# Low parts of 34 expert blocks made beside the mixers and kept in DRAM; the delta heads' inverse by transposes

## The chip, the core and the metric

The kernel runs on one core of one Trainium2 chip. The metric is device microseconds of one execution. TensorE (PE) multiplies matrices, VectorE (DVE) and ScalarE (ACT) work elementwise, GpSimd (POOL) and SyncE (SP) mainly issue DMAs here, and all DMAs run on the core's 16 DMA engines. Each engine takes its instructions strictly in order, and so does the queue in which SP or POOL issues DMAs: an issue that waits holds back every issue behind it.

## The reference, cut to what matters

One decoder layer for 544 tokens (512 of a prompt, 32 of samples). Two token mixers run on the projections of the normalised input; one of them, the gated delta rule, solves a unit triangular system for each chunk and head. Then comes a product-key expert layer with 16,384 experts of one neuron each.

```python
def gated_delta_recurrence(q, k, v, g, beta, s0):
    ...
        lmat = jnp.where(strict, bt[..., :, None] * gam * kk, 0.0)
        rhs = bt[..., None] * (vc.transpose(0, 2, 1, 3) - eg[..., None] * ks)
        u = lax.linalg.triangular_solve(eye + lmat, rhs, left_side=True, lower=True,
                                        unit_diagonal=True)

def peer_ffn(h, peer_wq, peer_keys, expert_u, expert_v):
    ...
        idx = ia * N_KEYS + ib                       # 128 experts chosen for each token
        gate = jax.nn.softmax(s_top, axis=-1)
        u = expert_u[idx]
        act = jax.nn.gelu(jnp.einsum('nd,nhkd->nhk', hb, u).astype(F32))
        wgt = (gate * act).astype(hb.dtype)
        return jnp.einsum('nhk,nhkd->nd', wgt, expert_v[idx])
```

## The kernel before, in words

**High and low parts.** A float32 matrix that TensorE is to multiply is split into a high part `whi` (rounded to the matmul's format) and a low part `wlo` (the rest), and a product is made of three matmuls: high by high, high by low, low by high. `wload` (lines 125 to 135) loads a block of 128 x 1024 through SP into `wraw`, ACT copies it to `whi` (line 120), and DVE subtracts to get `wlo` (line 121). `wsum` (lines 136 to 145) spares DVE: ACT writes `whi` (line 142) and then minus `whi` into `wlo` (line 143), and a DMA that POOL issues (line 144) adds the block from DRAM onto it once more.

**Mixers (83 to about 540 us).** The loop over the four heads (line 746 on) steps three generators side by side: `mix_a` (HGRN2 head), `mix_b` (delta head) and a filler that makes the next head's projections (`proj`, the matmuls of line 153) or the gates. What each step emits is then ordered on the engines by a scheduler; `order` rows below show the outcome. In `mix_b`, `inverse` builds the inverse of I + L for four chunks at once by doubling: at each of six levels, L times XT (line 532) is masked into ZT (533), then X times ZT (536) is subtracted from XT (540), and, except at the last level, ZT times X (539) is subtracted from X (542). XT is the transpose of X all along. All these are float32 matmuls of 128 x 128, and their PSUM tiles come from a pool `mb` of two buffers.

**Early expert blocks (750 to about 1140 us).** The expert inputs `eu` are 128 blocks of 128 experts. For 384 of the tokens the kernel computes all activations densely: `dots_u` makes 24 matmuls of 384 columns per block (lines 931, 932, 934) into `pu`. 62 blocks run early: the first 28 (`NPRE`) stay in SBUF, and 34 (`NSP`, every second block from 29 on) are stored to DRAM (`asp`, line 946) and read back later. All 62 take their weights through `wsum`, with three `wraw` and four `whi` and `wlo` buffers. Up to 922 us this runs beside the top-16 selection, which is DVE work; then `gates_of` (lines 1027 to 1056) builds, for 12 groups of 32 tokens, a dense map of the gates: one-hot tiles `oa` and `ob` on DVE and ACT, their product `pg` on TensorE (1048), a copy to `go` on ACT (1050, two buffers), a product on DVE (1052), and four DMAs that SP issues to store `go` into `gdram` (1056). Between them, rows of `eur` and `ev` for the other tokens are gathered by indirect DMAs that POOL issues (1073), and DVE multiplies them (1081, 1091).

**Product phase (1190 to 1970 us).** The remaining 66 blocks and all products with `ev` (line 1159).

The order of the expert part is that of a scheduler that simulates the engines; the mixers' order comes from a scheduler too.

Of the kernel before, what the change touches and what calls it, by code (L numbers as in the profile page):

```python
# [18 lines left out]
T = 544  # L19
# [17 lines left out]
NH2 = 4  # L37
NSP = 34
SEL = (0, 1, 2, 4, 3)
LATE = 127  # L40
XL, NYO = 118, 6
TW = 3, 2
# [9 lines left out]

@with_exitstack
def step_kernel(ctx: ExitStack, tc: tile.TileContext, xT, pT, pk, wab, win, wbr, wout, wq, keysT, eu, eur, ev,
                wple, wpg, sh, sd, scv, yT, o_hp, o_dp, o_cv, o_hs, o_ds, gdram, ysp, gsp, x1s, asp):
    nc = tc.nc
    V, S, G, PE = nc.vector, nc.scalar, nc.gpsimd, nc.tensor

# [77 lines left out]
    def wsum(src):  # L136

        raw = wr.tile([128, 1024], F32, name="wraw", tag="wraw", bufs=NRAW)
        nc.sync.dma_start(raw, src)
        hi = wp.tile([128, 1024], F32R, name="whi", tag="whi", bufs=NHI)  # L140
        lo = wp.tile([128, 1024], F32R, name="wlo", tag="wlo", bufs=NHI)
        S.activation(hi, raw, AF.Copy)
        S.activation(lo, hi.bitcast(F32), AF.Copy, scale=-1.0)
        G.dma_start(lo, src, accum_op=OP.add)
        return hi.rearrange("p (k c) -> p k c", c=128), lo.rearrange("p (k c) -> p k c", c=128)

    def mm3(ps, pairs, halves=(0, 1)):
# [322 lines left out]
    def mix_b(h):  # L470
# [36 lines left out]
        def bc(mk, n):  # L507
            return mk[:, None, :].to_broadcast([128, 4, 128]) if n == 4 else mk[:NS, :NS]

        def inverse(Lm, X, XT, ZT, n, levels):  # L510
            def each(f):
                if n == 4:
                    for c in range(4):
                        f(lambda t: t[:, c])
                else:
                    f(lambda t: t)

            def ps():
                p = p4()
                return p if n == 4 else p[:NS, 0, :NS]  # L520

            idt = ident if n == 4 else ident[:NS, :NS]
            p = ps()
            each(lambda at: PE.transpose(at(p), at(Lm), idt))
            V.tensor_mul(ZT, p, bc(maskf[1], n))
            V.tensor_sub(XT, bc(ident, n), ZT)
            V.tensor_mul(X, Lm, bc(m1l, n))
            V.tensor_sub(X, bc(ident, n), X)
            yield
            for m in levels:  # L530
                p = ps()
                each(lambda at: PE.matmul(at(p), at(Lm), at(XT), start=True, stop=True))  # L532
                V.tensor_mul(ZT, p, bc(maskf[m], n))
                yield
                p2 = ps()
                each(lambda at: PE.matmul(at(p2), at(X), at(ZT), start=True, stop=True))  # L536
                if m != levels[-1]:
                    p3 = ps()
                    each(lambda at: PE.matmul(at(p3), at(ZT), at(X), start=True, stop=True))
                V.tensor_sub(XT, XT, p2)  # L540
                if m != levels[-1]:
                    V.tensor_sub(X, X, p3)
                yield

        X, XT, ZT = m4("m2"), m4("m3"), m4("m4")
# [130 lines left out]
    def gates(c0, n):  # L676
        for c in range(c0, c0 + n):
# [2 lines left out]
            G.dma_start(gsp[:, c], sg)  # L680
            yield

    def chain(*gs):
        for g_ in gs:
            yield from g_
# [58 lines left out]
    for h in range(NH):  # L744
# [6 lines left out]
        while any(alive):  # L751
# [3 lines left out]
            if i % FP[h] == 2 or not alive[1]:  # L755
                alive[2] = next(fill, 0) is None
            i += 1
    nc.sync.dma_start(o_cv, ncv)
    mixers.close()
    mp = yinA.enter_context(tc.tile_pool(name="mg", bufs=2, side="right", reuse_waits="tile"))  # L760
# [155 lines left out]


    acts = {}
    spilled = [NPRE + 1 + 2 * i for i in range(NSP)]
    early = list(range(NPRE)) + spilled  # L920
    act = ap_.tile([128, NPRE, ND], F32, name="act", bufs=1)
    slots = []
# [13 lines left out]

    def ublock_early(j):
        with tc.high_priority(offset=100000):
            wh, wl = wsum(eu[j])
        ps = dots_u(wh, wl)  # L940
        a = act[:, j] if j < NPRE else stored(j)
        S.activation(a, ps[:, :ND], AF.Gelu_apprx_tanh)  # L942
# [387 lines left out]
             o_hs=(4, 128, 8, 128), o_ds=(4, 128, 8, 128))  # L1330


_SCR = dict(gdram=(128, NGQ, ND // 32, 128), ysp=(128, 8, T), gsp=(128, 16, T), x1s=(5, 128, 8, 128), asp=(NSP, 128, ND))


def unlay(np, r):
# [27 lines left out]
```

## Time and profile before

| | us |
|---|---|
| median of three runs (2071.32 to 2079.03) | 2077.46 |
| the profiled execution's own time | 2075.1 |
| its span | 2073.3 |
| mixers, 83 to 540: PE, DVE, ACT busy | 455.22, 339.26, 245.11 of 457 |
| selection, 770 to 920: PE, DVE busy | 147.30, 149.86 of 150 |
| gate maps, 922 to 1188: PE, DVE, ACT busy | 231.60, 224.08, 166.81 of 266 |
| product phase, 1190 to 1970: PE busy | 780.00 of 780 |

The page lists busy time, idle time and its releaser for each engine. A view of stretches gives, for a stretch of the span, each engine's busy time, the granted clock of TensorE (1.00 is its upper level), the mean busy share of the 16 DMA engines and GB/s. A DMA share slightly over 1 is one in which the engines were never without a packet. A matmul's duration overlaps its successor's; its price is the distance between two starts.

### The profile page before, as it was taken

The page shows a single profiled execution, that of the slowest core. Times are in us where ns is not written, and L with a number is a line of the kernel's source. Part 1 is how long each engine was busy: PE and PEld are TensorE (multiplying, and loading weights), DVE is VectorE, ACT ScalarE, POOL GpSimd, SP SyncE. Part 2 cuts the span into 40 slices and gives each one's busy share as a digit, 9 for nine tenths or more (in the row PEclk, how much of TensorE's full clock was granted, in tenths as well). Part 3 has the DMA queues.
Part 4 walks back from the last instruction along what each step waited for, and adds up shares of the span by engine and source line. Part 5 has one row for each costly group of instructions (what it writes and reads, how often), then busy time and mean ns, then how long its engine had stood idle before and what let it go on. Part 6 is the DMA issues. An engine that isn't in the chain of part 4 may idle for free.

```text
span 2073.3 us, 34544 instructions
## 1 busy us (share of the span) xinstructions
PE 1981.1 (96%) x12372; PEld 1841.1 (89%) x12372; DVE 1677.8 (81%) x4534; ACT 1004.9 (48%) x1660; POOL 547.4 (26%) x537
## 2 busy tenths in 40 slices
PE   6999999999998999998989799999999999999986
PEld 6899999998997999998989688888888888888886
DVE  7776968785566999998889898888888888887877
ACT  5646465643344357765767333333333333333374
POOL 0001010101000001134444455543434343443500
PEclk9999999999998999999999899999999999999998
DMA  4112131222754259999999999999999998999843
GB/s 150 62 42 83 59 106 47 89 89 92 270 178 138 78 123 242 241 280 325 304 324 329 309 357 340 337 352 345 347 341 350 331 344 329 337 337 335 292 133 105
DMA packets 178573, 480.46 MB, mean 232 GB/s; under 512 B 17376, under 2 KB 70624, under 8 KB 178272
## 3 DMA queue, kind: packets, MB, share of 16 engines
q1 hardware_dynamic: 117264, 257.63, 36.2%
q0 software_dynamic: 61136, 220.62, 33.0%
q8 instruction: 97, 1.59, 0.3%
q14 instruction: 76, 0.62, 0.1%
HBM read 435.82 MB, written 42.37 MB: 231 GB/s over the span
## 4 chain that ended last, share of the span: by engine, by line
PE 80%; issue 5%; DVE 5%; DMA 4%; ACT 3%; SPq 2%; POOL 0%; DVEq 0%; ACTq 0%; POOLq 0%
PE pacc L1159 25%; PE pj L153 14%; PE pu L931 7%; PE pu L932 7%; PE pu L934 7%; PE pj L881 4%; PE pj L1268 2%; SPq L1056 2%; PE pg L1048 2%; DMA gdram<-go 1%; PE pma L336 1%; PE pmb L532 1%; PE pmb L536 1%; DMA rows<-in_ev,idxs 1%; PE psc L902 1%
## 5 line engine op out<-in xcount | busy, mean ns | idle before, releaser
L931 PE MATMUL pu<-hh,whi 128*128 128x384 f32 x1024 | 346.8, 339 | 9.5 <-ACT acts L942 6.8
L932 PE MATMUL pu<-hl,whi 128*128 128x384 f32 x1024 | 346.0, 338 | 0.0
L1073 POOL DMA_INDIRECT rows<-in_ev,idxs x160 | 219.1, 1369 | 260.0 <-DVE accg L1091 221.3
L120 ACT ACTIVATE whi<-wraw 128x1024 fp32r<-128x1024 f32 x172 | 181.5, 1056 | 192.8 <-PE pj L153 93.7
L121 DVE TENSOR_TENSOR wlo<-wraw,whi 128x1024 fp32r<-128x1024 f32 x172 | 209.9, 1221 | 79.6 <-ACT whi L120 67.9
L1073 POOL DMA_INDIRECT rows<-in_eur,idxs x160 | 206.1, 1288 | 241.3 <-DVE jk L1081 192.5
L1091 DVE SCALAR_TENSOR_TENSOR accg<-rows,wts,accg 128x1024 f32<-128x1024 f32 x158 | 202.2, 1280 | 14.9 <-DMA rows<-in_ev,idxs 14.5
L931 PEld LDWEIGHTS pu<-hh,whi 128*128 128x128 f32 x1024 | 193.1, 189 | 13.3 <-ACT acts L942 7.1
L934 PE MATMUL pu<-hh,wlo 128*128 128x384 f32 x1024 | 204.5, 337 | 0.0
L1159 PE MATMUL pacc<-whi,wgl 128*128 128x512 f32 x768 | 197.3, 392 | 4.7 <-DVE wgl L121 4.6
L1159 PE MATMUL pacc<-whi,wgh 128*128 128x512 f32 x768 | 197.8, 393 | 3.7 <-ACT wgh L120 3.7
L1159 PE MATMUL pacc<-wlo,wgh 128*128 128x512 f32 x768 | 195.5, 390 | 0.0
L932 PEld LDWEIGHTS pu<-hl,whi 128*128 128x128 f32 x1024 | 193.1, 189 | 2.5
L121 DVE TENSOR_TENSOR wlo<-vraw,whi 128x1024 fp32r<-128x1024 f32 x128 | 156.5, 1222 | 41.8 <-ACT whi L120 34.2
L120 ACT ACTIVATE whi<-vraw 128x1024 fp32r<-128x1024 f32 x128 | 134.6, 1053 | 94.3 <-PE pacc L1159 81.7
L934 PEld LDWEIGHTS pu<-hh,wlo 128*128 128x128 f32 x1024 | 179.1, 188 | 0.0
L1159 PEld LDWEIGHTS pacc<-whi,wgl 128*128 128x128 f32 x768 | 144.7, 189 | 37.1 <-DVE wgl L121 5.8
L153 PE MATMUL pj<-xh,whi 128*128 128x272 f32 x768 | 175.3, 301 | 1.3 <-ACT xh L120 1.3
L153 PE MATMUL pj<-xl,whi 128*128 128x272 f32 x768 | 171.2, 296 | 0.2 <-DVE xl L121 0.2
L1159 PEld LDWEIGHTS pacc<-wlo,wgh 128*128 128x128 f32 x768 | 144.5, 188 | 30.1
L1159 PEld LDWEIGHTS pacc<-whi,wgh 128*128 128x128 f32 x768 | 143.6, 188 | 30.4 <-ACT wgh L120 3.8
L153 PE MATMUL pj<-xh,wlo 128*128 128x272 f32 x768 | 169.7, 297 | 0.7 <-DVE wlo L121 0.7
(484 smaller groups left out, 4294.3 us busy)
## 6 DMA issues: line engine op xcount, KB each, us to landing
wraw<-in_eu SPq DMA_DIRECT2D x128, 512.0 KB
vraw<-in_ev SPq DMA_DIRECT2D x128, 512.0 KB
wlo<-in_eu POOLq DMA_DIRECT2D x62, 512.0 KB
wraw<-in_win SPq DMA_DIRECT2D x48, 512.0 KB
gg<-gdram SPq DMA_DIRECT2D x25, 768.0 KB
gdram<-go SPq DMA_DIRECT2D x36, 512.0 KB
wraw<-in_wout SPq DMA_DIRECT2D x16, 512.0 KB
wraw<-in_wq SPq DMA_DIRECT2D x16, 512.0 KB
```

The costliest lines, as they stand in the source:

```text
L120: S.activation(hi, src, AF.Copy)
L121: return V.tensor_sub(lo, src, hi.bitcast(F32))
L153: PE.matmul(ps[:, hf, :HT], a, b[:, HS[hf]], start=(i == 0 and j == 0), stop=(i == n - 1 and j == 2))
L881: PE.matmul(p[:, i, :HT], w_[:, k], x_[:, k, :HT], start=(k == 0 and j == 0), stop=(k == 7 and j == 2))
L931: PE.matmul(ps[:, :ND], wh[:, k], hh[:, k], start=(k == 0), stop=False)
L932: PE.matmul(ps[:, :ND], wh[:, k], hl[:, k], start=False, stop=False)
L934: PE.matmul(ps[:, :ND], wl[:, k], hh[:, k], start=False, stop=(k == 7))
L1048: PE.matmul(p[:, j], A[:, j], B[:, j], start=True, stop=True)
L1056: nc.sync.dma_start(gdram[:, q:min(q + 8, NGQ), ch], gv[:, q:min(q + 8, NGQ)])
L1073: G.indirect_dma_start(out=r, out_offset=None, in_=src, in_offset=bass.IndirectOffsetOnAxis(ap=idx, axis=0))
L1091: V.scalar_tensor_tensor(accs[i], r, wts[i][:, k:k + 1], accs[i], op0=OP.mult, op1=OP.add)
L1159: PE.matmul(pacc[t][:, hf], w_[:, ts], v_[:, hf * 512:(hf + 1) * 512], start=(j == 0 and i == 0), stop=(j == 127 and i == 2))
```

## The change

It has two parts. First, a new generator `lows` is stepped once at the end of every turn of the mixers' loop. For each of the 34 spilled blocks it loads the block into `lraw` (SP), makes the high part of each half on ACT and subtracts it in place on DVE, and stores the low part to a new DRAM tensor `usp` (SP). Its steps are spread by `LOWS`. The 34 blocks then take their weights through `wread`, which loads `whi` as before but reads `wlo` from `usp` by a plain DMA on SP. The first 28 blocks keep `wsum`. Second, `inverse` no longer multiplies ZT by X: at each level but the first, X is made by transposing XT on TensorE and copying it out of PSUM on ACT.

```diff
@@ -37,6 +37,8 @@
+SPILLED = [NPRE + 1 + 2 * i for i in range(NSP)]
+LOWS = (2, 1, 2, 2)
@@ -142,6 +144,16 @@
+    def wread(src, low):
+
+        raw = wr.tile([128, 1024], F32, name="wraw", tag="wraw", bufs=NRAW)
+        nc.sync.dma_start(raw, src)
+        hi = wp.tile([128, 1024], F32R, name="whi", tag="whi", bufs=NHI)
+        lo = wp.tile([128, 1024], F32R, name="wlo", tag="wlo", bufs=NHI)
+        S.activation(hi, raw, AF.Copy)
+        nc.sync.dma_start(lo.bitcast(F32), low)
+        return hi.rearrange("p (k c) -> p k c", c=128), lo.rearrange("p (k c) -> p k c", c=128)
@@ -530,16 +542,16 @@
             for m in levels:
                 p = ps()
                 each(lambda at: PE.matmul(at(p), at(Lm), at(XT), start=True, stop=True))
+                if m != levels[0]:
+                    p3 = ps()
+                    each(lambda at: PE.transpose(at(p3), at(XT), idt))
                 V.tensor_mul(ZT, p, bc(maskf[m], n))
+                if m != levels[0]:
+                    S.activation(X, p3, AF.Copy)
                 yield
                 p2 = ps()
                 each(lambda at: PE.matmul(at(p2), at(X), at(ZT), start=True, stop=True))
-                if m != levels[-1]:
-                    p3 = ps()
-                    each(lambda at: PE.matmul(at(p3), at(ZT), at(X), start=True, stop=True))
                 V.tensor_sub(XT, XT, p2)
-                if m != levels[-1]:
-                    V.tensor_sub(X, X, p3)
                 yield
@@ -679,6 +691,26 @@
+    def lows():
+
+        raw = mp.tile([128, 1024], F32, name="lraw", bufs=1)
+        for i, j in enumerate(SPILLED):
+            nc.sync.dma_start(raw, eu[j])
+            for _ in range(LOWS[0]):
+                yield
+            for c in (slice(0, 512), slice(512, 1024)):
+                hi = mp.tile([128, 512], F32R, name="lhi", tag="lhi", bufs=1)
+                split(hi, raw[:, c].bitcast(F32R), raw[:, c])
+                for _ in range(LOWS[1]):
+                    yield
+            for _ in range(LOWS[2] - LOWS[1]):
+                yield
+            nc.sync.dma_start(usp[i], raw)
+            for _ in range(LOWS[3]):
+                yield
+
+    low = lows()
@@ -755,6 +787,9 @@
             i += 1
+            next(low, None)
+    for _ in low:
+        pass
@@ -936,7 +971,7 @@
     def ublock_early(j):
         with tc.high_priority(offset=100000):
-            wh, wl = wsum(eu[j])
+            wh, wl = wsum(eu[j]) if j < NPRE else wread(eu[j], usp[spilled.index(j)])
```

SP's queue in the first head's mixers, before (`win` are projection weights, `s0a` a state):

```order
L128 DMA wraw<-in_win 128x1024 x2
L320 DMA s0a<-in_sh 128x1024
L128 DMA wraw<-in_win 128x1024 x12
L473 DMA s0b<-in_sd 128x1024
L128 DMA wraw<-in_win 128x1024 x5
```

and the same place now (line numbers are those of the changed kernel):

```order
L130 DMA wraw<-in_win 128x1024 x2
L332 DMA s0a<-in_sh 128x1024
L699 DMA lraw<-in_eu 128x1024
L130 DMA wraw<-in_win 128x1024
L709 DMA usp<-lraw 128x1024
L130 DMA wraw<-in_win 128x1024
L699 DMA lraw<-in_eu 128x1024
L130 DMA wraw<-in_win 128x1024
L709 DMA usp<-lraw 128x1024
L699 DMA lraw<-in_eu 128x1024
```

Between the weight loads stand a load of a block, which waits for the store before it, and a store, which waits for DVE's second half.

TensorE's queue at one level of a delta head's inverse, before (`m` tiles are L, X, XT and ZT, `b` the head's q and k):

```order
L532 MATMUL pmb<-m_1073,m_1004 128x128 x4
L575 MATMUL pmb<-b_755,b_826 128x128 x4
L536 MATMUL pmb<-m_1074,m_1072 128x128 x4
L153 MATMUL pj<-xh,wlo 128x272
L539 MATMUL pmb<-m_1072,m_1074 128x128 x4
```

and now:

```order
L544 MATMUL pmb<-m_1078,m_1006 128x128 x4
L547 MATMUL pmb<-ident,m_1078 128x128 x4
L165 MATMUL pj<-xh,wlo 128x272 x2
L165 MATMUL pj<-xh,whi 128x272 x2
L587 MATMUL pmb<-b_755,b_826 128x128 x4
L553 MATMUL pmb<-m_1079,m_1077 128x128 x4
```

The four matmuls behind the level's second product are gone, and four transposes (with `ident`) stand behind its first.

SP's queue where the gate maps begin, before:

```order
L139 DMA wraw<-in_eu 128x1024 x41
L1056 DMA gdram<-go 128x8x128 x3
L1056 DMA gdram<-go 128x128
L139 DMA wraw<-in_eu 128x1024 x3
L1056 DMA gdram<-go 128x8x128 x3
L1056 DMA gdram<-go 128x128
```

and now:

```order
L156 DMA wlo<-usp 128x1024
L1091 DMA gdram<-go 128x8x128 x3
L1091 DMA gdram<-go 128x128
L152 DMA wraw<-in_eu 128x1024
L156 DMA wlo<-usp 128x1024
L152 DMA wraw<-in_eu 128x1024
L156 DMA wlo<-usp 128x1024
L1091 DMA gdram<-go 128x8x128 x2
L156 DMA wlo<-usp 128x1024
L152 DMA wraw<-in_eu 128x1024
L1091 DMA gdram<-go 128x8x128
L1091 DMA gdram<-go 128x128
```

The low parts' reads, which POOL issued before, now stand among the stores of the gate maps.

## Rows read from the trace of the kernel before

**Rows 1.** The page's slices of the span, busy tenths in 40 slices.

```profile
PE   6999999999998999998989799999999999999986
DMA  4112131222754259999999999999999998999843
```

**Rows 2.** Stretches: length, engines' busy time and instructions, clock, DMA share, GB/s.

```profile
83.00:540.00 457.00, 455.22 (x3459) 423.35 (x3457) 339.26 (x564) 245.11 (x387) 35.60 (x87) 0.99 0.26 87
770.00:920.00 150.00, 147.30 (x854) 146.16 (x853) 149.86 (x1484) 108.36 (x138) 32.99 (x41) 1.00 0.98 243
922.00:1137.00 215.00, 195.07 (x1313) 193.66 (x1312) 181.66 (x460) 145.85 (x332) 95.30 (x92) 0.96 1.05 321
1137.00:1188.00 51.00, 36.53 (x196) 32.48 (x195) 42.42 (x93) 20.96 (x47) 22.17 (x15) 0.80 0.92 302
1190.00:1970.00 780.00, 780.00 (x3785) 689.56 (x3784) 651.51 (x814) 281.94 (x382) 346.08 (x266) 1.00 0.93 338
```

**Rows 3.** TensorE's longest wait from 83 to 540: total us, times, longest.

```profile
PE pj L153 <- ACT whi L120: 1.2, 1, 1.2
```

**Rows 4.** Timeline of TensorE in the mixers: start us, us, instruction, count.

```profile
442.53 1.06 PE L539 MATMUL pmb<-m,m 128*128 128x128 f32 x8
443.43 0.61 PE L336 MATMUL pma<-QL,KL 128*128 128x128 f32 x4
...
444.63 0.60 PE L261 MATMUL pmb<-ident,b 128*128 128x128 f32 x4
444.98 0.37 PE L153 MATMUL pj<-xh,wlo 128*128 128x272 f32 x1
```

**Rows 5.** Groups by form, 83 to 540: busy us, mean ns, idle before.

```profile
L121 DVE TENSOR_TENSOR wlo<-wraw,whi 128x1024 fp32r<-128x1024 f32 x40 | 48.7, 1218 | 30.5 <-ACT whi L120 25.1 <-PE pmb L536 3.6 <-PE pj L153 1.8
L120 ACT ACTIVATE whi<-wraw 128x1024 fp32r<-128x1024 f32 x41 | 43.2, 1056 | 59.0 <-PE pj L153 43.3 <-issue 15.6
L542 DVE TENSOR_TENSOR m<-m,pmb 128x512 f32<-128x512 f32 x20 | 13.7, 683 | 1.3 <-PE pmb L539 1.0
L262 ACT ACTIVATE bt<-pmb 128x512 f32<-128x512 f32 x8 | 4.8, 597 | 3.8 <-PE pmb L261 3.6
```

**Rows 6.** SP's waits from 83 to 434.

```profile
SPq L128 <- DVE wlo L121: 226.0, 22, 20.6
```

**Rows 7.** DMA from 770 to 920: packets, MB, share; issues, count, KB each.

```profile
q0 software_dynamic: 5110, 18.45, 65.6%
q1 hardware_dynamic: 4890, 17.81, 32.0%
...
wraw<-in_eu SPq DMA_DIRECT2D x35, 512.0 KB
wlo<-in_eu POOLq DMA_DIRECT2D x35, 512.0 KB
asp<-acts POOLq DMA_DIRECT2D x6, 192.0 KB
```

**Rows 8.** DMA from 922 to 1186.

```profile
q0 software_dynamic: 12750, 45.35, 57.5%
q1 hardware_dynamic: 44388, 37.86, 44.5%
...
wlo<-in_eu POOLq DMA_DIRECT2D x24, 512.0 KB
```

**Rows 9.** Waits from 922 to 1188.

```profile
POOL wlo L144 <- ACT wlo L143: 30.3, 13, 12.2
...
DVE act L1052 <- ACT go L1050: 25.4, 4, 8.5
...
ACT go L1050 <- DMA gdram<-go: 21.9, 3, 10.8
...
DVE accg L1091 <- DMA rows<-in_ev,idxs: 6.9, 2, 3.8
DVE jk L1081 <- DMA rows<-in_eur,idxs: 5.6, 3, 3.9
```

More of the change, by code (lines that the diff above doesn't have):

```diff
@@ L54, in step_kernel @@
 def step_kernel(ctx: ExitStack, tc: tile.TileContext, xT, pT, pk, wab, win, wbr, wout, wq, keysT, eu, eur, ev,
-                wple, wpg, sh, sd, scv, yT, o_hp, o_dp, o_cv, o_hs, o_ds, gdram, ysp, gsp, x1s, asp):
+                wple, wpg, sh, sd, scv, yT, o_hp, o_dp, o_cv, o_hs, o_ds, gdram, ysp, gsp, x1s, asp, usp):
     nc = tc.nc
@@ L918, in step_kernel @@
     acts = {}
-    spilled = [NPRE + 1 + 2 * i for i in range(NSP)]
+    spilled = SPILLED
     early = list(range(NPRE)) + spilled
@@ L1330 @@
              o_hs=(4, 128, 8, 128), o_ds=(4, 128, 8, 128))
-_SCR = dict(gdram=(128, NGQ, ND // 32, 128), ysp=(128, 8, T), gsp=(128, 16, T), x1s=(5, 128, 8, 128), asp=(NSP, 128, ND))
+_SCR = dict(gdram=(128, NGQ, ND // 32, 128), ysp=(128, 8, T), gsp=(128, 16, T), x1s=(5, 128, 8, 128), asp=(NSP, 128, ND),
+            usp=(NSP, 128, 1024))
 def unlay(np, r):
```

## Prediction

> **What bounds the kernel now.** I read the slices first, then the stretches, then in each stretch the waits. The slices [rows 1] show TensorE nearly full all along but for a dip in the middle, and DMA full from there on. The stretches [rows 2] name the limits. From 83 to 540, in the mixers, TensorE is busy 455 of 457 us while DVE has 118 us free and ACT 212; its longest wait on anything is 1.2 us [rows 3], so this stretch is worth what its matmuls cost. From 770 to 920, in the selection, TensorE (147 of 150) and DVE (150 of 150) are both full. From 922 to 1188, in the gate maps, nothing that computes is full: TensorE has 232 of 266 us, DVE 224, but DMA has a share of 1.05 until 1137 and 0.92 after that. There the waits end at DMA [rows 9]: ACT's copies to `go` wait 21.9 us for the stores to `gdram` to free a buffer, DVE waits 25.4 us for those copies, and 12.5 us (5.6 + 6.9) for gathered rows. From 1190 to 1970 TensorE is full again. So work taken off TensorE counts in the mixers, work taken off DMA counts from 922 to 1188, and nearly nowhere else.
>
> **The inverse.** There are 4 heads and 5 levels at which X is renewed, 20 places. At each, four float32 matmuls, which the trace shows as 8 records, go, and four transposes come. The 8 records hold TensorE for 0.90 us (442.53 to 443.43), and the four transposes of an existing line, 4 records, for 0.35 us (444.63 to 444.98) [rows 4]; by the step of 0.11 us of the matmul's records (0.90 / 8) it would be 0.45. So a place saves 0.45 to 0.55 us; I take 0.45, for all 20: -9 us, on the path, as TensorE is the limit. DVE loses 20 subtractions of 683 ns, 13.7 us, and ACT gains 20 copies of about 597 ns, 12 us [rows 5]. The chain of a level gets shorter by one DVE step too, but TensorE did not wait for it. The two `mb` buffers stay two per level. What is late next is TensorE's own remaining work.
>
> **Low parts beside the mixers.** 34 blocks in halves give 68 roundings on ACT and 68 subtractions on DVE. No row has the half form of the subtraction; half of the full form is 609 ns and the 512-wide subtraction from PSUM takes 683 [rows 5], so DVE gains 41 to 46 us; ACT, at 528 to 597 ns, gains 36 to 41. With the inverse, DVE goes from 339 to about 369 and ACT from 245 to about 296 in a stretch of some 450: 82% and 66%. Both still have room, so by load alone the price is nothing. But all engines work in order, so each half step can stand 0.6 us ahead of something that TensorE needs, and an ACT step waits for DVE to give back the one `lhi` buffer. The price therefore lies between 0 (the cover of TensorE's independent projections is enough, as it now is: 1.2 us of waiting) and 44 us (both DVE halves of every block, 34 x 2 x 0.65, fall on the path). The scheduler puts the steps into gaps, and the row of waits is near nothing today, so I take 4.
>
> The DMAs: 34 loads and 34 stores of 512 KB. A plain one costs 1.37 us of all engines (below), so 93 us more, which takes the share from 0.26 to about 0.47. On SP, a store now waits for DVE and a load for the store before it, with projection weights queued behind both. SP already spends 226 us of 351 waiting for a `wraw` buffer to be given back [rows 6], and TensorE's and ACT's waits in the mixers name no landing of weights; three buffers cover a delay of some microseconds. I put this at nothing; without that cover it is part of the second rival's range.
>
> **The read back.** First the prices. From 770 to 920, POOL's queue moves 35 accumulating DMAs and six stores of 192 KB in 65.6% of 150 us, 98.4 us, and SP's queue 35 plain loads of the same 512 KB in 32.0%, 48.0 us [rows 7]. A plain load costs 48.0 / 35 = 1.37 us; the six stores at that rate 3.1; an accumulating DMA (98.4 - 3.1) / 35 = 2.72. The low part's plain read from `usp` is not in the trace; it has the size and shape of a `wraw` load, so I take 1.37, with 2.72 as its upper bound. Ten of the 34 blocks fall before 922, where DMA is not the limit: nothing. The other 24 [rows 8] fall into the gate maps. DMA work there is now 57.5% + 44.5% of 264 us, 269 us, and falls by 24 x 1.35 = 32 to 237. ACT loses 24 copies of 1.06 us and POOL 24 issues, for which it waited 30.3 us with gathers queued behind [rows 9]. The queue of SP gains 24 reads, each waiting for TensorE to free a `wlo` buffer, with stores of `gdram` behind it.
>
> How far does the stretch of 266 us shrink? With no idle DVE it would be 224; without the DMA waits of DVE (25.4 + 12.5) it would be 228; by DMA work it would be 237. All three engines would then stand above 94%, in a stage in which each waits for the others in turn, and from 1137 on the stage is led by DVE, with DMA already below 1. So I give back a quarter to a half of the 32 us: 248, a gain of 18 us (bounds 0 and 38). After that the product phase is full of TensorE work and passes the gain on unchanged.
>
> **Sum.** -9 + 4 - 18 = -23 us. Against the profiled 2075.1 this is 2052; the median of the runs lies 2.4 higher, so 2054. A measurement of this kernel can tell about 0.5%, 10 us, from no change.
>
> **Rivals.**
> *More relief.* The DMA waits of DVE go altogether and the gate maps take 228 us: -9 + 4 - 38 = -43, 2034. For it: the stores to `gdram` are what ACT waits for, and gathers are freed on POOL too. Against it: TensorE and DVE at 100% in a stage of crossed waits.
> *The read back buys nothing.* The packet times of an accumulating DMA may be mostly waiting inside its queue, not use of the engines; then 1.35 us per block are no saving, the stage stays at 266, and -9 + 4 gives 2072, within 0.5%. Against it: from 770 to 920 the two shares add up to 0.98 at 243 GB/s, while from 1190 on a share of 0.93 moves 338 [rows 2, 7], so the accumulating packets do seem to use up engine time. The Trainium skill has a rule on this side: DMA: Bandwidth & Descriptors, "Issuing engines are not separate DMA queues", says that DMAs of all issuers run on the same 16 engines, so that a change of issuer saves only the issuing time. By that rule the move from POOL to SP alone would give this rival's 2072; no run here yet shows a plain DMA of POOL beside one of SP.
> *The mixers get crowded.* The slower side: DVE's half steps fall on TensorE's path. At the full 44 us the sum is -9 + 44 - 18 = +17, 2094; it decides once the price passes about 37 us (then 2088), that is, 28 of the 34 blocks. For it: DVE at 82% and in order. Against it: hardly a wait today [rows 3], and the load.
> *SP's order.* The 24 reads wait in SP for TensorE, and stores of `gdram` and weights wait behind them. If SP inherits the 30 us that POOL waited for its low parts [rows 9] and the gate maps lengthen by that, -9 + 4 - 18 + 30 = +7, 2084, the same within 0.5%. For it: two `go` buffers whose stores come late already. Against it: four `wlo` buffers, and the reads stand several blocks ahead of their use. The same page of the Trainium skill, in "Queues, rings and completion order", says that each DMA engine serves the queues by turns; by that the reads would compete with the `gdram` stores in one queue rather than with gathers, which is on this rival's side and gives no other number.
>
> **How the numbers follow.** Forecast (2044 to 2064): 0.50. More relief: 0.13. Read back buys nothing: 0.16. SP's order: 0.11. Crowded mixers: 0.10. Faster by over 0.5% (below 2067) are the first two, 0.63; within 0.5% the next two, 0.27; slower 0.10. The range goes from the relief rival's 2034 to 2080, which leaves out the crowded mixers and the worse half of SP's order.
>
> **What would show it.** In the new profile: TensorE in the mixers ends about 9 us earlier, with its waits still near zero and DVE near 82%; a row of waits of TensorE on DVE or ACT of over 10 us there speaks for crowding. From 770 to 920 the stretch keeps its length. In the gate maps the share of POOL's queue falls by more than that of SP's rises, ACT's wait for `gdram` falls below 10 us, and the stage takes about 248. If the stage keeps 266 with a DMA share still at 1, the price of the accumulating DMA was wrong; if SP's waits on TensorE grow there, it was the order.

## The result: 0.9% faster, by two wrong sizes of opposite sign

The changed kernel takes 2057.37 us (median of 5 runs, 2055.6 to 2062.17) against 2079.03 for the kernel before on the same chip (5 runs). The recorded ratio is 0.9912, 95% interval [0.9897, 0.9926]; the two medians alone would give 0.9896, and in the larger samples below the kernel before has medians from 2075.35 to 2077.57. The forecast was 2054. Its profiled execution took 2059.39 us with a span of 2057.6, 15.7 less than before (2073.3). Where the 15.7 us are is read from the first start of three matmuls on TensorE in both traces (`pj<-mh`, the projection behind the mixers; `pg`, the first product of the gate maps; `pacc`, the first of the product phase). Before (duration in ns, min/median/max, then first and last start in us):

```profile
L153 PE MATMUL pj<-mh,whi x128: 284/288/372, 587.6 to 637.3; 128*128 128x272 f32 x128
L1048 PE MATMUL pg<-ob,oa x768: 270/275/579, 929.1 to 1166.6; 128*128 128x128 f32 x192
L1159 PE MATMUL pacc<-whi,wgh x768: 387/389/632, 1170.5 to 1968.3; 128*128 128x512 f32 x192
```

and after:

```profile
L165 PE MATMUL pj<-mh,whi x128: 284/289/374, 602.8 to 652.5; 128*128 128x272 f32 x128
L1083 PE MATMUL pg<-ob,oa x768: 270/276/552, 942.7 to 1151.9; 128*128 128x128 f32 x192
L1194 PE MATMUL pacc<-whi,wgh x768: 386/390/795, 1154.6 to 1954.1; 128*128 128x512 f32 x192
```

| stretch | before | after | difference | forecast |
|---|---|---|---|---|
| start to first `pj<-mh` (the mixers) | 587.6 | 602.8 | +15.2 | -9 + 4 = -5 |
| to first `pg` (output projections, selection) | 341.5 | 339.9 | -1.6 | 0 |
| `pg` to first `pacc` (the gate maps) | 241.4 | 211.9 | -29.5 | -18 |
| to the end of the span | 902.8 | 903.0 | +0.2 | 0 |

So in these two profiles the mixers lost 15 us where 5 were to be gained, and the gate maps gave 30 where 18 were expected. (The 15 hold a part that differs by some 8 us from one profile to another; see the table of the experiments.)

The stretches of the kernel after (length, busy time and instructions of PE, PEld, DVE, ACT and POOL, granted clock, DMA share, GB/s; they answer to [rows 2]):

```profile
83.00:554.00 471.00, 461.79 (x3446) 426.79 (x3445) 366.98 (x608) 294.90 (x475) 38.95 (x92) 0.98 0.44 152
784.00:934.00 150.00, 147.42 (x856) 146.61 (x855) 149.86 (x1486) 98.89 (x128) 24.75 (x31) 1.00 0.94 249
936.00:1120.00 184.00, 184.00 (x1291) 184.00 (x1290) 179.18 (x453) 124.86 (x306) 63.34 (x66) 1.00 1.02 364
1120.00:1171.00 51.00, 35.88 (x202) 32.18 (x201) 43.08 (x97) 20.47 (x47) 18.75 (x15) 0.80 0.90 297
1173.00:1953.00 780.00, 780.00 (x3785) 689.75 (x3784) 649.40 (x811) 282.74 (x383) 353.88 (x267) 1.00 0.94 339
```

**Gate maps.** The first 215 us of [rows 2] became 184, in which TensorE now shows no gap at all; the 51 us behind them hold the same work as before (35.88 us of TensorE, before 36.53). The selection and the product phase kept their length (150 and 780). What the DMA engines do in the selection, 784 to 934 (packets, MB, share of 16 engines; then issues, count, KB each, median us to landing; answers to [rows 7]):

```profile
q0 software_dynamic: 3945, 14.13, 50.8%
q1 hardware_dynamic: 6321, 23.04, 43.0%
...
wraw<-in_eu SPq DMA_DIRECT2D x35, 512.0 KB, 5.7
wlo<-in_eu POOLq DMA_DIRECT2D x25, 512.0 KB, 7.1
wlo<-usp SPq DMA_DIRECT2D x10, 512.0 KB, 6.2
asp<-acts POOLq DMA_DIRECT2D x6, 192.0 KB, 6.0
```

Here the price can be read side by side: 35 + 10 plain DMAs in 43.0% of 150 us are 1.43 us each, and with 3.2 us for the six `asp` stores the 25 accumulating ones come to (76.2 - 3.2) / 25 = 2.92 us each. The prices of the forecast (1.37 and 2.72) held to 4% and 7%, and for the read back the lower bound. In the gate maps, 936 to 1171 (answers to [rows 8]):

```profile
q1 hardware_dynamic: 47776, 50.19, 62.8%
q0 software_dynamic: 8980, 31.72, 36.4%
```

That is 99.2% of 235 us, 233 us of DMA work; forecast were 237. From the 269 us before, 36 went. ACT's wait for the stores to `gdram` [rows 9: 21.9 us] has no row any more.

**Mixers.** What TensorE waited for from 83 to 554 (total us, times, longest; before, the longest was 1.2 [rows 3]):

```profile
PE pj L165 <- ACT sg L691: 2.7, 1, 2.7
PE pmb L513 <- DVE b L500: 1.5, 1, 1.5
```

No wait is long, but there are eleven of them. The longest one in the order of time (start us, us, engine, line, instruction; in brackets the idle time ahead of it and what ended it):

```profile
440.84 0.63 ACT L122 ACTIVATE lhi<-lraw 128x512 fp32r<-128x512 f32 x1 [3.74 <-DMA lraw<-in_eu]
...
441.38 1.04 ACT L122 ACTIVATE whi<-wraw 128x1024 fp32r<-128x1024 f32 x1
...
442.43 1.28 ACT L691 ACT_TABLE_LOAD   x1
...
443.73 0.62 ACT L691 ACTIVATE sg<-pj 128x544 f32<-128x544 f32 x1
...
444.40 0.60 PE L165 MATMUL pj<-xh,whi 128*128 128x272 f32 x1 [2.67 <-ACT sg L691]
```

ACT stands 3.74 us for the landing of a block (`lraw`) that nobody is in a hurry for. Behind that half step in its order is `sg`, which empties the `pj` that TensorE is to fill next; so TensorE stands 2.67 us. At 57 us the same happens: ACT stands 2.85 us for a block, and TensorE 2.19 us for the step behind it. These two are 4.9 of the 15.0 us that TensorE is idle from 38 to 588 us. Another 2.7 are a wait at 74 us that the kernel before has too (2.4). And 1.8, from 552 to 557, point to SP's order: TensorE waits there for the mixers' outputs, which are read again through `yr`, whose first load SP issues at 544.7, right behind the last store of a low part (544.4), which waited for DVE's half step; before, it was issued at 517.0. The other 5.6 us, in nine waits, were not followed one by one.

Behind the longest wait the clock falls (stretches, columns as above):

```profile
430.00:443.70 13.70, 11.74 (x92) 11.29 (x90) 13.15 (x13) 9.48 (x13) 1.08 (x2) 1.00 0.55 181
443.80:450.60 6.80, 6.20 (x28) 5.89 (x28) 4.81 (x10) 3.37 (x5) 0.54 (x1) 0.50 0.40 159
```

For 6.8 us TensorE has 1.2 GHz instead of 2.4, after having stood; that is another 3 us or so of work not done. But the same standing does not bring this each time: in a profile of a kernel with the same mixers (ACT's copy put back, below) TensorE stood 2.34 us at this place, and the clock stayed at 1.00 from 430 to 460 us. Six rows over the whole of the mixers give the sum of idle time and clock, here after:

```profile
38.00:145.00 107.00, 101.85 (x786) 95.29 (x785) 76.51 (x169) 64.32 (x106) 3.95 (x14) 0.97 0.34 118
145.00:250.00 105.00, 103.01 (x776) 94.27 (x774) 90.46 (x155) 71.89 (x116) 10.18 (x23) 1.00 0.41 140
250.00:350.00 100.00, 96.60 (x712) 88.21 (x711) 83.30 (x134) 71.70 (x113) 9.60 (x23) 0.98 0.41 144
350.00:450.00 100.00, 97.33 (x701) 89.47 (x701) 80.61 (x129) 66.22 (x107) 8.95 (x21) 0.95 0.44 155
450.00:545.00 95.00, 95.00 (x714) 88.36 (x713) 60.47 (x100) 43.01 (x73) 7.76 (x15) 0.98 0.52 181
545.00:588.00 43.00, 41.21 (x311) 40.27 (x310) 27.12 (x35) 16.27 (x22) 1.08 (x2) 0.96 0.83 282
```

and before:

```profile
38.00:145.00 107.00, 104.33 (x832) 98.36 (x831) 75.31 (x166) 57.72 (x95) 3.37 (x14) 1.00 0.20 62
145.00:250.00 105.00, 105.00 (x794) 97.33 (x793) 84.60 (x143) 59.37 (x96) 9.76 (x23) 0.98 0.22 70
250.00:350.00 100.00, 99.99 (x748) 92.91 (x748) 78.85 (x136) 63.42 (x97) 7.66 (x23) 0.98 0.25 84
350.00:450.00 100.00, 100.00 (x763) 92.44 (x762) 80.31 (x130) 56.90 (x92) 9.25 (x22) 1.00 0.25 84
450.00:545.00 95.00, 93.31 (x710) 87.15 (x709) 50.98 (x72) 34.85 (x54) 8.66 (x16) 1.00 0.43 150
545.00:588.00 43.00, 43.00 (x347) 43.00 (x347) 27.10 (x36) 12.43 (x15) 0.00 (x0) 1.00 0.61 193
```

In each row, the length less PE's busy time is idle, and the length times (1 - clock) is work lost to the clock. After: 15.0 us idle, 13.8 lost to the clock. Before: 4.4 and 4.1. What remains of the time from 38 us to the first `pj<-mh` is TensorE's work at full clock: 541.1 before and 536.0 after. So the +15.2 is -5.1 of work, +10.6 of idle and +9.7 of clock. (The clock has two digits, so it and the work are good to some 2 us.) DVE at 367 of 471 us and ACT at 295 are just what the forecast worked out (369 and 296): the engines are not full, and the loss isn't one of load alone.

### The profile page after: what moved, and what is told of

Read it like the earlier page. It is cut to its first block, busy times and chain, and to the rows that moved or that the text cites. A ratio compares the mean times of both kernels' runs of the same rounds, so it can differ in the third digit from the quotient of the medians.

```text
span 2057.6 us, 34634 instructions
## 1 busy us (share of the span) xinstructions
PE 1976.0 (96%) x12292; PEld 1833.5 (89%) x12292; DVE 1706.7 (83%) x4582; ACT 1028.8 (50%) x1717; POOL 513.9 (25%) x503
## 4 chain that ended last, share of the span: by engine, by line
PE 86%; DVE 5%; DMA 4%; ACT 3%; issue 3%; POOL 0%; SPq 0%; DVEq 0%; ACTq 0%; POOLq 0%
PE pacc L1194 26%; PE pj L165 15%; PE pu L967 8%; PE pu L966 8%; PE pu L969 8%; PE pj L916 5%; PE pg L1083 3%; PE pj L1303 2%; DMA lraw<-in_eu 1%; PE pma L348 1%; PE pmb L553 1%; PE pmb L544 1%; ACT whi L122 1%; PE psc L937 1%; DMA usp<-lraw 1%
## 5 line engine op out<-in xcount | busy, mean ns | idle before, releaser
L123 DVE TENSOR_TENSOR wlo<-wraw,whi 128x1024 fp32r<-128x1024 f32 x172 | 210.0, 1222 | 74.6 <-ACT whi L122 65.7
L165 PE MATMUL pj<-xh,wlo 128*128 128x272 f32 x768 | 174.9, 302 | 0.0
L1194 PEld LDWEIGHTS pacc<-wlo,wgh 128*128 128x128 f32 x768 | 144.7, 188 | 30.1
```

Of the source, the lines that this page charges most:

```text
L123: return V.tensor_sub(lo, src, hi.bitcast(F32))
L165: PE.matmul(ps[:, hf, :HT], a, b[:, HS[hf]], start=(i == 0 and j == 0), stop=(i == n - 1 and j == 2))
L1194: PE.matmul(pacc[t][:, hf], w_[:, ts], v_[:, hf * 512:(hf + 1) * 512], start=(j == 0 and i == 0), stop=(j == 127 and i == 2))
```

## The experiments

All times are medians, and each ratio is to runs of the kernel before on the same chip. The columns between are from one profile each, read as above; the last adds up the waits of ACT and DVE on the tiles of the half steps (the rounding on ACT and the subtraction on DVE of half a block) from 38 to 590 us. In the texts of what was expected, wq's end is the end of the query projection, which follows the output projections and ends 180 us or so behind the first `pj<-mh`.

| kernel | us | ratio to before [95%] | first `pj<-mh` | PE idle | clock | work | half steps' waits |
|---|---|---|---|---|---|---|---|
| before | 2075 to 2079 | 1 | 587.6 | 4.4 | 4.1 | 541.1 | |
| after | 2057.37 | 0.9912 [0.9897, 0.9926] | 602.8 | 15.0 | 13.8 | 536.0 | 49.5 |
| new inverse alone | 2074.62 | 0.9991 [0.9981, 1.0002] | 589.7 | 7.4 | 10.2 | 534.1 | |
| former inverse | 2071.43 | 0.9978 [0.9966, 0.9989] | 607.5 | 16.4 | 9.0 | 544.0 | 51.3 |
| read back alone | 2051.43 | 0.9879 [0.9862, 0.9896] | 592.9 | 3.8 | 11.2 | 539.9 | |
| half steps alone | 2051.61 | 0.9888 [0.9871, 0.9905] | 591.3 | 10.9 | 9.2 | 533.2 | 32.3 |
| transfers alone | 2046.76 | 0.9868 [0.9843, 0.9893] | 585.5 | 7.4 | 6.1 | 534.0 | |
| both, not linked | 2052.97 | 0.9884 [0.9866, 0.9902] | 594.4 | 11.3 | 9.8 | 535.3 | 31.7 |
| load further ahead | 2064.67 | 0.9949 [0.993, 0.9969] | 606.1 | 17.5 | 15.5 | 535.1 | 51.6 |
| two half buffers | 2061.83 | 0.9938 [0.9915, 0.9961] | 605.6 | 16.5 | 18.2 | 532.9 | 63.8 |
| three half buffers | 2072.73 | 0.999 [0.9978, 1.0003] | 612.4 | 23.4 | 17.2 | 533.7 | 93.3 |
| read back by POOL | 2058.89 | 0.9922 [0.99, 0.9944] | 602.1 | 14.8 | 13.8 | 535.5 | 48.4 |
| ACT's copy put back | 2060.07 | 0.9919 [0.9897, 0.994] | 593.8 | 14.7 | 5.3 | 535.8 | 42.3 |
| low parts by POOL | 2117.46 | 1.0201 [1.0177, 1.0226] | 666.1 | 62.1 | 40.4 | | |

Two of these kernels (read back by POOL, ACT's copy put back) have the mixers of the kernel after. Their PE idle agrees with it to 0.3 us; the clock's loss does not: 13.8, 13.8 and 5.3. So of the two losses the idle time is the kernel's, and of the clock's a single profile tells only to some 8 us. That is also why the first `pj<-mh` of one profile alone proves little here.

### The three parts of the change, one at a time

**The new inverse alone** (before, with only the `inverse` part of the diff).

> The kernel before with the new inverse alone; no low parts in the mixers, the 34 spilled blocks made by the accumulating transfer as before. If the transposes save what the sum said (20 places x 0.45 us), the first projection of the delta outputs stands about 9 us earlier than before (587.6 to about 578.6) and the time is about 2070 us. Rival: the transposes are themselves part of the mixers' loss of 14 us, or are hidden anyway: 2079 us or more.

Measured 2074.62, a ratio of 0.9991 [0.9981, 1.0002]: hardly a gain. The transposes themselves are cheap: in the kernel after, the four of a level take 118.40 to 118.76, 0.36 us, where the eight records took 0.90 [rows 4]:

```profile
118.40 0.60 PE L547 MATMUL pmb<-ident,m 128*128 128x128 f32 x4
118.76 0.49 PE L165 MATMUL pj<-xh,wlo 128*128 128x272 f32 x2
```

And TensorE's work fell by 7 us (541.1 to 534.1), as it is 533 to 536 in every kernel of the table with the new inverse that has a number there, and 540 to 544 with the former. (The last row has none: its losses are too large for this reckoning.) But 3 us came back as idle time (4.4 to 7.4), and 6 as clock in this profile. The price of the step was nearly right; that all of it would reach the end was not. Why TensorE waits more here was not tested.

**The former inverse in the kernel after** (that part of the diff undone).

> The changed kernel with the former inverse; low parts and read back stay. If the transposes save 9 us in the changed kernel too, its time is about 2066 us, and the mixers, which end 14 us later than before in the changed kernel, end about 23 us later here. If the transposes take part in the loss, 2045 to 2052 us.

Measured 2071.43. Against the kernel after that is 0.9978 to 0.9912, some 14 us (with about 4 either way, from the two intervals), more than the 9 of the step. TensorE's work is 8 us longer (544.0 to 536.0). The rest isn't settled: the new inverse also takes 20 subtractions off DVE, the engine that the low parts load, but no run here separates that.

**The read back alone** (the former inverse, one block's low part made, read back for all 34).

```diff
-        for i, j in enumerate(SPILLED):
+        for i, j in enumerate(SPILLED[:1]):
-            wh, wl = wsum(eu[j]) if j < NPRE else wread(eu[j], usp[spilled.index(j)])
+            wh, wl = wsum(eu[j]) if j < NPRE else wread(eu[j], usp[0])
```

> The former inverse; the low part of one spilled block alone is made in the mixers, and all 34 spilled blocks read that one back, so the values of 33 blocks are wrong; the traffic of the gate maps is the changed kernel's. If the whole gain of 31 us in the gate maps is the price of the read back against the accumulating transfer, the stage takes about 235 us and the time is about 2048 us with the mixers where they were before (wq's end at 770). If part of the 31 us comes from something else of the change, the stage takes about 248 us, as the sum had it, and the time is about 2061 us.

Measured 2051.43, faster than the whole change. The instructions on `pg` and `pacc` (duration min/median/max, first and last start):

```profile
L1083 PE MATMUL pg<-ob,oa x768: 271/275/550, 933.3 to 1142.5; 128*128 128x128 f32 x192
L1194 PE MATMUL pacc<-whi,wgh x768: 387/389/796, 1145.3 to 1946.9; 128*128 128x512 f32 x192
```

933.3 to 1145.3 is 212.0 us, as in the kernel after (211.9) and not 241.4 as before. So the 30 us of the gate maps belong to the read back, whatever the mixers do. The low parts in the mixers cost 2071.43 - 2051.43 = 20 us by the two kernels with the former inverse.

### Kind or issuer, DMA or ACT

**The read back issued by POOL.**

```diff
-        nc.sync.dma_start(lo.bitcast(F32), low)
+        G.dma_start(lo.bitcast(F32), low)
```

> The changed kernel with the plain read back issued by POOL in place of SP; nothing else differs. If the kind of the transfer sets its price (a plain write takes 1.43 us of all engines, an accumulating one 2.92), the gate maps keep their 211 us between the first pg and the first pacc (942.7 to 1154.6) and the time stays at 2055 to 2060. If the price follows the issuing engine and its queue, the stage goes back to about 240 us and the time to about 2085.

Measured 2058.89; `pg` to `pacc` is 941.9 to 1154.2, 212.3 us. DMA from 935 to 1170:

```profile
q0 software_dynamic: 12479, 44.42, 49.9%
q1 hardware_dynamic: 44333, 37.72, 49.0%
...
wlo<-usp POOLq DMA_DIRECT2D x24, 512.0 KB
```

Compare [rows 8]: the same queue, the same 24 transfers, nearly the same bytes (45.35 to 44.42 MB), and 117 us of engine time in place of 152: 1.4 us less for each. The kind of the transfer sets the price; the issuer does not. Nor is it POOL's freed order that shortened the stage: here POOL waits 40.9 us for TensorE to free a `wlo` buffer (936 to 1171 us), more than the 30.3 us for ACT before [rows 9], with the gathers behind it, and the stage keeps its 212 us. By the Trainium skill (DMA: Bandwidth & Descriptors, "Issuing engines are not separate DMA queues") a change of issuer saves only issuing time. The trace agrees: SP or POOL, 212 us. But the rule was no reason for the rival that the forecast hung on it, since the change altered the kind too.

**ACT's needless copy put back** ahead of each read back.

```diff
         S.activation(hi, raw, AF.Copy)
+        S.activation(lo, hi.bitcast(F32), AF.Copy, scale=-1.0)
         nc.sync.dma_start(lo.bitcast(F32), low)
```

> The changed kernel with ACT's second copy, the one that the read back made needless, put back ahead of each of the 34 read backs; its result is overwritten by the read back. If the gate maps gained 30 us because the DMA engines have less to do, the stage from the first pg to the first pacc stays at 211 to 214 us and the time at 2056 to 2061. If it is the time that ACT was given back (34 copies, some 24 of them in the stage, about 1 us each), the stage grows to 225 to 235 us and the time to 2070 to 2080.

Measured 2060.07. `pg` starts at 935.6 and `pacc` at 1150.3: 214.7 us, 3 more than without the copy. So at most 3 of the 30 us are ACT's; the rest is DMA work. By the forecast's prices 32 us of it were taken away, by the shares of the two traces 36 (269 to 233), and 30 came out.

### What the mixers lose

**Half steps alone, transfers alone.** The first loads and stores one block once, lets the 68 half steps run on that buffer, and reads this one low part back for all 34 blocks; the second has all transfers and no half step.

```diff
-            nc.sync.dma_start(raw, eu[j])
+            if i == 0:
+                nc.sync.dma_start(raw, eu[j])
...
-            nc.sync.dma_start(usp[i], raw)
+            if i == 0:
+                nc.sync.dma_start(usp[i], raw)
```

> The changed kernel with the half steps of ACT and DVE alone: one block is loaded and stored once, the 68 half steps then run on that buffer without any transfer, and the read back reads that one block, so the values of 33 blocks are wrong. If ACT's waiting in order for the landing of a block (18.3 us in 11 waits), or the traffic, is what costs the mixers, they end about where the transposes alone put them: wq's end near 762 to 770 and a time of about 2035 to 2043 us. If the half steps' own time on ACT and DVE (68 x 0.63 and 68 x 0.69 us) is what costs, wq's end stays near 782 and the time near 2055 us.

```diff
-                hi = mp.tile([128, 512], F32R, name="lhi", tag="lhi", bufs=1)
-                split(hi, raw[:, c].bitcast(F32R), raw[:, c])
```

> The changed kernel with the loads and stores of the 34 blocks in their order and no half steps; the raw block is stored in place of its low part, so the low parts of the spilled blocks are wrong. With the half steps alone the mixers ended at 774.1 (wq's end), with both at 784.2, with the transposes alone at 771.0. If the traffic and SP's waiting between a load and its store delay the mixers' own loads, wq's end stays near 782 and the time near 2056 us. If it takes ACT's waiting in order for a landing, which is gone here because no engine reads the block, wq's end falls to 770 to 775 and the time to about 2047 to 2052 us.

Measured 2051.61 and 2046.76. The transfers alone cost nothing that shows: PE idle is 7.4 us as with the new inverse alone, though SP waits 105.5 us for landings and 74.6 for stores:

```profile
SPq L707 <- DMA lraw<-in_eu: 105.5, 31, 5.7
SPq L699 <- DMA usp<-lraw: 74.6, 30, 4.8
```

So the cover that the forecast named for SP, three `wraw` buffers, holds. The half steps alone cost 3.5 us of idle (10.9) and by the ratios some 4 us of time (0.9868 to 0.9888, with intervals that overlap), so they came out between the two times that were expected. The larger of their waits from 38 to 590 us:

```profile
ACT lhi L122 <- DVE lraw L123: 24.5, 25, 2.5
```

This is ACT waiting for DVE to give back the one `lhi`.

**Both, not linked.** The half steps read a tile that is always there, and the transfers go on beside them.

```diff
-                split(hi, raw[:, c].bitcast(F32R), raw[:, c])
+                S.activation(hi, xh[:, 0, :512].bitcast(F32), AF.Copy)
+                V.tensor_sub(hi, xh[:, 0, :512].bitcast(F32), hi.bitcast(F32))
```

> The changed kernel with the loads, the stores and the half steps all there, but without a link between them: the half steps read a tile that is in the SBUF all the time (xh) and write into their own small tile, and the stores write the raw block, so the low parts of the spilled blocks are wrong. Steps alone ended wq at 774.1, transfers alone at 766.7, both linked at 784.2. If the link is the cause (ACT and DVE in order behind a landing, SP in order behind a half step), this comes to 770 to 776 and about 2046 to 2052 us. If it is the load of both together on engines and memory, it stays at 781 to 786 and 2054 to 2060 us.

Measured 2052.97, between the two ranges and nearer the first; idle 11.3, as the half steps alone. Linked, the same work takes 2057.37 with 15.0 of idle. So it isn't the load of both together; the link costs the difference, 3.7 us of idle, and the half steps in themselves about as much. In time that is some 4 to 6 us, but the two intervals just meet at 0.99.

**The load further ahead.** `LOWS` at (4, 1, 1, 1).

> The changed kernel with the four step counts at 4, 1, 1, 1 in place of 2, 1, 2, 2: a block's load is issued four scheduler steps ahead of its first half step, and its store right behind the second. If ACT's 18.3 us of waiting for landings is the cause, that wait nearly goes, wq's end comes to 774 to 778 and the time to 2048 to 2052 us. If the traffic is the cause, no change: 2055 to 2059. If SP's wait for a store before the next load (65.8 us in 28 waits) holds the mixers' loads, which are now closer behind, it becomes slower: 2060 or more.

**Two half buffers** in the room of the one, each loaded four to five steps ahead; the core of the edit:

```diff
+        raws = [load(0)]
+        yield
+        raws.append(load(1))
+        yield
+        for n, (i, j, c) in enumerate(halves):
+            raw = raws[n]
+            hi = mp.tile([128, 512], F32R, name="lhi", tag="lhi", bufs=1)
+            split(hi, raw.bitcast(F32R), raw)
+            yield
+            nc.sync.dma_start(usp[i][:, c], raw)
...
+            if n + 2 < len(halves):
+                raws.append(load(n + 2))
```

> The changed kernel with two buffers of half a block in the room of the one: each half is loaded four to five steps ahead of its half step, while the other half is still in use; 68 loads and 68 stores of half the size. If ACT's in-order wait is the cause: wq's end 772 to 778 and 2046 to 2052 us, the best of these. If the traffic is the cause: 2055 to 2059. If it is SP's turns (twice as many transfers, each store waiting for its half step), 2060 or more.

Measured 2064.67 and 2061.83, both slower than the kernel after. Neither took ACT's wait for landings away: it is 13.0 us in the first and 23.9 in the second, from 18.3. With two half buffers, though the loads stand further ahead in the program:

```profile
ACT lhi L122 <- DMA lraw<-in_eu: 23.9, 13, 4.5
DVE lraw L123 <- ACT lhi L122: 19.0, 11, 4.9
ACT lhi L122 <- DVE lraw L123: 16.7, 13, 2.5
```

In both, SP waited longer for DVE's half steps than in the kernel after, 97.2 us, since a store stands closer behind the step that makes it: 122.0 us with the load further ahead, and 121.1 with two half buffers, where a load also waited 86.9 us for stores (65.8 in the kernel after). What was gained in steps was lost in SP's order. So these runs did not test the wait for the landing; the next one takes most of it away.

**Three half buffers**, each loaded two halves ahead; to fit, the half step is cut into two quarter steps with an `lhi` of 256 columns.

```diff
+            raw = mp.tile([128, 512], F32, name="lraw", tag="lraw", bufs=3)
...
+            for q in (slice(0, 256), slice(256, 512)):
+                hi = mp.tile([128, 256], F32R, name="lhi", tag="lhi", bufs=1)
+                split(hi, raw[:, q].bitcast(F32R), raw[:, q])
+                yield
+            nc.sync.dma_start(usp[i][:, c], raw)
+            yield
+            if n + 3 < len(halves):
+                raws.append(load(n + 3))
```

> The changed kernel with three buffers of half a block, each loaded two halves (some six to eight scheduler steps) ahead of its use, and the half step cut into two quarter steps so that it fits into the room. If ACT's waiting in order for landings is what the link between transfers and steps costs, that wait (18.3 us in 11 waits, 23.9 in 13 with two half buffers) is gone, wq's end comes to 775 to 780 and the time to 2049 to 2054 us, with 1 to 4 us of it for the fixed cost of twice as many steps. If the link costs through ACT and DVE waiting for each other at every step, or through SP's turns, the wait for landings goes and the time stays at 2057 or more.

Measured 2072.73, no better than the kernel before. The waits, 38 to 590 us:

```profile
ACT lhi L122 <- DVE lraw L123: 66.0, 68, 3.7
DVE lraw L123 <- ACT lhi L122: 19.9, 27, 2.4
ACT lhi L122 <- DMA lraw<-in_eu: 6.8, 4, 2.4
```

The wait for landings fell from 18.3 to 6.8 us, but with 136 steps through one `lhi` ACT now waits 66 us for DVE, SP's wait for DVE's steps rose to 144.7 us (97.2 in the kernel after), and PE idle rose to 23.4. So less waiting for landings is not enough; what the landings alone cost stays open, since the other waits grew. Among the kernels with the new inverse and half steps on ACT and DVE, idle nearly always rises with the sum of these waits: 31.7 and 32.3 go with 11.3 and 10.9; 42.3, 48.4 and 49.5 with 14.7, 14.8 and 15.0; 51.6 with 17.5; 63.8 with 16.5; 93.3 with 23.4. That is about 0.2 us of TensorE for each further us in which ACT or DVE stands in its order for a half step; from the 7.4 without any half step it is 0.1 to 0.2. This is a fit to eight runs, three of them with the same mixers, not a cause shown one by one; a second `lhi` buffer would test it, and wasn't tried.

**Low parts by POOL alone**, loads and stores too.

```diff
-            nc.sync.dma_start(raw, eu[j])
+            G.dma_start(raw, eu[j])
...
-                split(hi, raw[:, c].bitcast(F32R), raw[:, c])
+                G.tensor_copy(hi, raw[:, c])
+                G.tensor_sub(raw[:, c].bitcast(F32R), raw[:, c], hi.bitcast(F32))
...
-            nc.sync.dma_start(usp[i], raw)
+            G.dma_start(usp[i], raw)
```

> The changed kernel with the low parts made by POOL alone: copy and subtraction of each half step, the load and the store of each block are all POOL's, which is busy for some 42 of the mixers' 550 us; ACT, DVE and SP have nothing of it. The floor is what the transposes and the read back give together with mixers without low parts, about 2046 us (the run with the transfers alone gave 2046.8). If the load of half steps on DVE and ACT and the link through their orders are the mixers' loss of about 11 us, this comes to 2046 to 2051 us and wq's end to 767 to 773. If POOL's own work in the mixers (kq, xp, hatt, waited for by DVE and PE) now stands behind the block's landings, or POOL's half steps slow DVE's, 2056 or more.

Measured 2117.46, slower than before by 2%. Waits, 38 to 590 us:

```profile
POOL lhi L704 <- DMA lraw<-in_eu: 117.1, 34, 5.0
POOL lraw L699 <- DMA usp<-lraw: 91.4, 33, 5.3
...
PE pmb L617 <- POOL kq L614: 26.3, 2, 16.1
```

POOL, idle for 93% of the mixers before, became the engine on which TensorE waits: its small copy `kq`, which TensorE needs, stood behind 208 us of landings of loads and stores, up to 16.1 us at once (26.3 of TensorE's 62.1 us of idle). An engine's idle time is not room if what little it does is urgent and its order is strict.

No version here beats the read back with free mixers (2046.76 with the transfers alone, where the low parts are wrong); the fastest kernel that makes all 34 low parts is the change itself.

## Right and wrong, by the steps of the prediction

- **What bounds the kernel: right.** TensorE's work counted in the mixers, DMA work in the gate maps, and the selection and the product phase passed everything on unchanged.
- **The inverse, -9: the price nearly right, the yield not.** TensorE's work fell by 5 to 8 us, but alone the part brought 2 us (between a gain of 4 and a loss of 0.4); 3 us were seen to go into new idle time. "What is late next is TensorE's own remaining work" failed there. Beside the low parts it was worth some 14, so the terms do not simply add up as the sum had them.
- **Low parts, +4 (bounds 0 to 44): the term mis-sized.** They cost 7.6 us of idle (7.4 to 15.0), and by the times 9 us with the new inverse (0.9868 to 0.9912) and 20 with the former (0.9879 to 0.9978). The load was forecast to 2 us; the step that failed was "by load alone the price is nothing" together with "The scheduler puts the steps into gaps". A small TensorE wait before [rows 3] said that there was no slack, not that there was much. That an ACT step waits for the one `lhi` was named in the prediction, and was given no price; it stands in the half steps' own part, about half of the loss. The other half is the link to the transfers, put at nothing. It was not late weights on SP, as the prediction asked; but at the end the `yr` loads came late behind the last store on SP (1.8 us of idle). The trace shows ACT standing for blocks that it could have had later (18.3 us), and of the link's two sides, ACT behind landings and SP behind half steps, neither was taken away alone. What the clock adds to the 7.6 us can't be told from single profiles.
- **The read back: price right, yield mis-sized.** 32 to 36 us of DMA work taken away gave 30, not 18. "I give back a quarter to a half" was the step: the prediction saw three engines above 94% and took from this that they would hold each other up. In the trace after, TensorE has 184.00 of 184 us and DVE 179.18. The long waits there [rows 9: 25.4 us of DVE for `go`, 21.9 of ACT for the stores to `gdram`] are gone with it. And the stretch from 1137 on, in which DMA was below 1, had nothing to lose: the last accumulating DMA before was issued at 1108.3.
- **The rivals.** *Read back buys nothing* fell by the run with POOL as issuer and by the prices in one trace. *SP's order* fell: SP's 23 reads stand among the stores, and TensorE has no gap. *Crowded mixers* came nearest to the mixers' mechanism, at a fifth to a half of its full price (9 to 20 of 44 us). *More relief* came nearer on the gate maps than the forecast (228 for the 266 us, 184 + 51 = 235 measured, the forecast 248), without the mixers' loss.
- **The whole**, 2054 for 2057.37, came out near by luck: in the profiles the mixers missed by +20 and the gate maps by -12, and the two errors have opposite signs.

## What to carry to other kernels

Filler work that is put in strict order ahead of urgent work can cost even where the engines have room: here idle rose with the time for which the filler steps stood, while their load stayed the same. What suggests itself, and was not shown here, is to give each such step its own buffers and to let its data have landed long before. Where DMA share is at 1 and every other engine waits in turn, count DMA work as the stage's length: what was taken from it here came back nearly whole (30 of 32 to 36 us). An accumulating DMA cost the engines twice a plain one of its size here (2.92 and 1.43 us), so a low part stored once and read back plainly pays where a stage that DMA bounds reads it, and where making it costs less than that (here 9 to 20 us in the mixers for 30).

## What was not expected of the hardware

- POOL's plain read back was as cheap as SP's: 1.4 us less for each than the accumulating DMA that POOL issued before, and 212 us for the stage either way.
- The clock's loss in the mixers was 13.8 us in one profile and 5.3 in another with the same mixers and the same idle time to 0.3 us, so single profiles of this kernel can't settle differences of some us.
- While POOL made the low parts, DVE's subtraction `KL<-ab` (line 379, 128 x 256, both inputs in the SBUF) took a mean of 643 ns from 60 to 500 us, where it takes 414 in the kernel after. The mean hides what happened: 12 of its 16 instances kept 0.41 us, and the three that started inside a subtraction of POOL took 1.50 to 1.52 us and ended no earlier than POOL's did (POOL from 355.30 for 1.35 us, DVE from 355.43 for 1.51). The Trainium skill (SBUF — State Buffer, "Who interferes with whom") says that a DVE instruction with two SBUF inputs contends with a GpSimd instruction that reads SBUF; the trace agrees. POOL's own subtraction took a mean of 1561 ns where DVE takes 682.
